# A decoder layer with three token mixers: one small statistics tile grows by 320 bytes, and the tiles allocated behind it move up by as much

## The chip, the core and the metric

The kernel runs on one core of a Trainium2 chip. The metric is the time of one execution on the device, in microseconds (us); lower is better. Before the change it is 323.63 us, the median of three runs (323.2 to 323.89).

## What is computed

One layer over 256 tokens of width 1024, in fp32. Cut to what matters:

```python
h = rmsnorm(x, g_in)
z = h @ w_in                      # one wide projection, then split
ya = moba_attention(rope(mq), rope(mk), mv);  ya = (ya * silu(mg)) @ w_up_moba
yb = dsa_attention(rope(dq), rope(dk), dv, rope(iq), rope(ik), iw);  yb = (yb * silu(dg)) @ w_up_dsa
yc = cross_attention(xq, *split(rmsnorm(mem, g_mem) @ w_mem_kv));    yc = (yc * silu(xg)) @ w_up_cross
g = sigmoid(glog + b_merge)       # three gates
out = rmsnorm(x + (g[0] * ya + g[1] * yb + g[2] * yc) @ w_out, g_final)
```

## The kernel before, in words

**Arithmetic.** Each fp32 operand of a matmul is split into a high and a low half in fp32r (`split_act`, L181 on, for x and mem; `split_weights`, L240 on, for weights), and each product is three matmuls: high by high, high by low, low by high (`product`, L251 on: L254, L255, L256; L280 in `gemm`). A matmul has a stationary operand (128 rows by 128 columns, loaded into TensorE by a LDWEIGHTS; the profile's PEld) and a moving operand that streams past it (128 to 512 columns).

**Order.** The work is a list of some 100 steps. Each step has one block of weights of up to 512 KB: loaded six steps ahead into a `wraw` tile (SP's DMA queue), split three steps ahead by ScalarE (L248, high half) and VectorE (L249, low half) into `whi` and `wlo` tiles, and used by the step's matmuls. The order of steps is written out by hand (`ORDER`), and everything that isn't a weight product (rope, attention, gates, statistics) is hung on a step by `at(...)`. TensorE and GpSimd follow the order of the program text.

**Which operand lies where.** In `gemm_t` (26 blocks of 48 matmuls), in the mq block (`gemm_k`, 96), the two xk blocks (`gemm_kv`, 96) and the up products (`gemm_u`, 12 blocks of 24) the weights are stationary and x, mem or a gated branch output moves, 256 columns at a time: 1248 + 96 + 96 + 288 = 1,728 matmuls. In `gemm` (mv, dv, xv, the two indexer blocks i0 and i1) and in the output product (`out_piece`) it is the other way round: x, mem or u is stationary and the weights move; 512 columns in mv, dv, xv and nearly all of the output product (216 matmuls in all), 264 and 320 in i0 and i1 (48 each).

**Addresses.** On-chip tiles live in pools that are laid out one behind another in the order in which they are opened: `const`, `raws` (raw x and weights), `ws` (split weights), `work` (temporaries), `keep` (the split x and mem, q, k, v, attention outputs, u and its halves). Within a pool each tag gets its slots when it is first used, each slot rounded up to 32 bytes. Counted per partition, this gives for the kernel before:

| what | start, bytes | behind a multiple of 512 |
|---|---|---|
| `cst` (constants, identity) | 16512 | 128 |
| `xr`, `wraw` (raw x, raw weights) | 27648, 35840 | 0 |
| `whi`, `wlo` (split weights) | 52224, 72704 | 0 |
| `nat` | 93184 | 0 |
| `xss` (8 bytes, a slot of 32) | 99328 | 0 |
| `sw` (swapped halves for rope; at the end g_final) | 99360 | 32 |
| `gate`, `t1`, `t2`, `ms` | 103648 to 117984 | 224 |
| `pr`, `pth`, `ptl` (probabilities and their split) | 121184 to 135008 | 352 |
| `xhi`, `xlo` and all else of `keep` | 138272 on | 32 |

The last tile of `keep` ends at byte 226848 of 229376. All `keep` tiles have sizes that are multiples of 512 bytes, so all begin 32 bytes behind a multiple of 512, and every 128-column block of one does as well. A split weight block begins at 0; in i0 (264 columns) its second half begins 1056 bytes on, at 32; in i1 (320 columns) 1280 bytes on, at 256.

**The lines around the change.** `start_stats` (L894 on) is hung on step 6. It squares the rows of x (already loaded into two `keep` tiles) and sums them into `sums`, a tile of two fp32 per partition with the tag `xss`; `rsqrt` (L211 on) turns them into the scale of each row. `sums` is written at L898 and read at L217 once, at 21.6 us.

Of the kernel before, what the change touches and what calls it, by code (L numbers as in the profile page):

```python
# [8 lines left out]
F32 = mybir.dt.float32  # L9
# [5 lines left out]
P = 128  # L15
# [95 lines left out]
def hybrid_layer_kernel(  # L111
# [18 lines left out]
    work = ctx.enter_context(tc.tile_pool(name="work", bufs=2))  # L130
# [83 lines left out]
    def rsqrt(r, ss, nm):  # L214

        v, sd, e = (work.tile([P, 2], F32, name=f"{nm}n{i}", tag=f"n{i}") for i in range(3))
        nc.vector.tensor_scalar(v, ss, 1.0 / D, EPS, op0=OP.mult, op1=OP.add)  # L217
        nc.scalar.activation(sd, v, AF.Sqrt)
        nc.vector.reciprocal(r, sd)
        nc.vector.tensor_tensor(e, r, r, op=OP.mult)  # L220
        nc.vector.tensor_tensor(e, e, v, op=OP.mult)
        nc.vector.tensor_scalar(e, e, -0.5, 1.5, op0=OP.mult, op1=OP.add)
        nc.vector.tensor_tensor(r, r, e, op=OP.mult)
# [668 lines left out]
            x_rows.append(rows)  # L892

    def start_stats():  # L894
        sums = work.tile([P, 2], F32, name="xss", tag="xss", bufs=1)
        for t in range(2):
            junk = work.tile([P, D], F32, name=f"xjunk{t}", tag="sw", bufs=1)
            nc.scalar.activation(junk, x_rows[t], AF.Square, accum_out=sums[:, t : t + 1])  # L898
        rsqrt(x_rstd, sums, "x")
        nc.vector.tensor_scalar_mul(xs_rstd, x_rstd, float(P**-0.5))  # L900
        nc.vector.tensor_copy(ident_r, ident)
        for t in range(2):
            nc.vector.tensor_scalar_mul(tab[:, t, :], tab0[:, t, :], x_rstd[:, t : t + 1])
# [13 lines left out]

    at(LOAD_ROWS, load_rows)
    at(X_STATS, start_stats)
    at(X_STATS, make_bias)  # L920
    at(X_STATS + 2, rstd_rows, x_rstd, rB, "rB")
# [147 lines left out]
```

## Time and profile before

| | |
|---|---|
| median of three runs | 323.63 us (323.2 to 323.89) |
| the profiled execution: its own time, its span | 324.77 us, 323.0 us |
| TensorE busy with matmuls / with weight loads | 313.0 us (97%) / 297.4 us (92%) |
| VectorE, ScalarE, GpSimd busy | 252.1, 202.9, 41.9 us |
| TensorE's granted clock | 0.999 of full |
| bytes moved by DMA, mean rate | 59.45 MB, 184 GB/s |

How to read it: a matmul's recorded duration (0.28 us for 256 columns) covers its way through the array, and the next one starts before it ends, so durations overlap. What one costs when they come back to back is the distance from its start to the next one's start, which the timeline gives to 0.01 us.

### The profile page before, as it was taken

To read this page: it belongs to the slowest core of one execution; us is meant where nothing else is said; L and a number is where in the kernel's file an instruction comes from. 1 tells how busy PE (TensorE), PEld (TensorE's weight loads), DVE (VectorE), ACT (ScalarE), POOL (GpSimd) and SP (SyncE) were. 2 spreads that over 40 slices of the span, in tenths; PEclk is the share of its full clock that TensorE was granted. 3 is DMA by queue.
4 is the path that set the end of the run, shared out by engine and by line. 5 is a ranking of instruction groups with operands and counts; after the bars stand their busy time and mean duration, and the time that the engine had idled before them with its cause. 6 is when DMAs were issued, how large, how long until landed. Compare 5 with 4: busy or idle time off the path is not lost.

```text
span 323.0 us, 6395 instructions
## 1 busy us (share of the span) xinstructions
PE 313.0 (97%) x2442; PEld 297.4 (92%) x2442; DVE 252.1 (78%) x458; ACT 202.9 (63%) x357; POOL 41.9 (13%) x58
## 2 busy tenths in 40 slices
PE   8899999998999999999999999999999999999992
PEld 7699999988999989879999999999999999998882
DVE  3579999899799999988766759998466775677523
ACT  5599674687878545577666588756444546643434
POOL 0001000017202000010200235321000111014011
PEclk9999999999999999999999999999999999999999
DMA  6989886864644446574443434478765666655003
GB/s 202 379 293 333 269 269 194 265 240 124 214 130 127 138 130 210 182 246 131 146 132 117 146 94 162 136 220 302 211 193 189 190 188 205 182 156 188 2 0 130
DMA packets 18368, 59.45 MB, mean 184 GB/s; under 512 B 2209, under 2 KB 2465, under 8 KB 18337
## 3 DMA queue, kind: packets, MB, share of 16 engines
q1 hardware_dynamic: 17760, 57.73, 57.1%
q10 hardware_dynamic: 576, 1.31, 1.0%
q8 instruction: 19, 0.31, 0.5%
q14 instruction: 13, 0.10, 0.1%
HBM read 55.89 MB, written 1.05 MB: 176 GB/s over the span
## 4 chain that ended last, share of the span: by engine, by line
PE 70%; DVE 15%; DMA 5%; ACT 4%; issue 4%; SPq 0%; ACTq 0%; DVEq 0%
DMA w3r<-w_in 3%; DVE wk L498 2%; DMA w25r<-w_in 2%; DVE m L496 1%; PE o_0ps L255 1%; PE o_0ps L256 1%; PE o_0ps L254 1%; DMA w0r<-w_in 1%; PE dya L642 1%; PE i_0ps L280 1%; PE i_1ps L280 1%; PE mv_1ps L280 1%; PE mv_0ps L280 1%; DVE acc L487 1%; PE lg L480 1%
## 5 line engine op out<-in xcount | busy, mean ns | idle before, releaser
L747 POOL TENSOR_TENSOR u<-u,gt 128x512 f32<-128x512 f32 x7 | 9.9, 1411 | 76.7 <-DVE gt L744 76.7
L616 POOL TENSOR_SCALAR dpr<-dpr,dst 128x128 f32<-128x128 f32 (+1 forms) x16 | 6.6, 425 | 84.1 <-DVE dst L614 83.9
L616 POOL TENSOR_SCALAR mpr<-mpr,mst 128x128 f32<-128x128 f32 (+1 forms) x16 | 9.8, 629 | 56.3 <-DVE mst L614 56.3
L734 ACT ACTIVATE gt<-gt,x_first 128x256 f32<-128x256 f32 x24 | 10.9, 501 | 2.7 <-DVE gt L731 2.5
L606 ACT ACTIVATE dpr<-dms,dst 128x128 f32<-128x128 f32 (+1 forms) x16 | 7.1, 446 | 3.6 <-DVE dst L602 3.6
L788 ACT ACTIVATE junk<-xn 128x512 f32<-128x512 f32 (+1 forms) x5 | 2.7, 543 | 8.6 <-DVE xn L786 8.6
L606 ACT ACTIVATE mpr<-mms,mst 128x128 f32<-128x128 f32 (+1 forms) x16 | 7.1, 444 | 1.2 <-DVE mst L602 1.2
L664 ACT ACTIVATE xpr<-xsc,xst,xs_rstd 128x256 f32<-128x256 f32 x8 | 4.4, 560 | 3.4 <-DVE xst L660 3.4
L752 ACT CAST us<-u 128x512 fp32r<-128x512 f32 x4 | 2.5, 624 | 6.2 <-POOL u L747 4.9
L647 ACT COPY dyT<-dya 64x256 f32<-64x256 f32 x8 | 2.9, 367 | 4.2 <-PE dya L642 4.1
L484 ACT ACTIVATE rl<-lg 128x384 f32<-128x384 f32 x8 | 3.9, 485 | 2.7 <-PE lg L480 1.6
L487 DVE SCALAR_TENSOR_TENSOR acc<-rl,iw,acc 128x128 f32<-128x128 f32 (+1 forms) x14 | 5.4, 431 | 0.1
L480 PE MATMUL lg<-ikT,iqT 128*128 128x128 f32 (+1 forms) x32 | 5.1, 282 | 0.1
L968 PE MATMUL warm<-ones 128*128 128x128 f32 x18 | 4.0, 419 | 1.1 <-DVE eps_t L963 1.1
L602 DVE CUSTOM_DVE_ANT_0 mms<-msc,bias_c 128x128 f32<-128x128 f32 (+1 forms) x16 | 5.0, 350 | 0.0
L968 PEld LDWEIGHTS warm<-ones 128*128 128x128 f32 x18 | 3.9, 328 | 1.1 <-DVE eps_t L963 1.1
L648 DVE TENSOR_TENSOR dyT<-dyT,dya 64x256 f32<-64x256 f32 x8 | 3.3, 417 | 1.8 <-ACT dyT L647 1.7
L628 ACT CAST dph<-dtp 128x384 fp32r<-128x384 f32 x8 | 3.8, 479 | 1.4 <-PE dtp L627 1.3
L629 DVE TENSOR_TENSOR dpl<-dtp,dph 128x384 fp32r<-128x384 f32 x8 | 4.4, 553 | 0.4
L602 DVE CUSTOM_DVE_ANT_0 dms<-dsc,sel 128x128 f32<-128x128 f32 (+1 forms) x16 | 4.7, 352 | 0.0
L786 DVE TENSOR_TENSOR xn<-o_0ps,xn 128x512 f32<-128x512 f32 x2 | 1.4, 691 | 4.2 <-PE o_0ps L256 4.2
L498 DVE MATCH_REPLACE8 wk<-m,wk 128x128 f32<-128x128 f32 (+1 forms) x14 | 4.7, 342 | 0.0
(1296 smaller groups left out, 1541.9 us busy)
## 6 DMA issues: line engine op xcount, KB each, us to landing
x_rows<-x SPq DMA_DIRECT2D x2, 512.0 KB, 8.7
eT<-memT SPq DMA_DIRECT2D x4, 256.0 KB, 4.6
xn<-x SPq DMA_DIRECT2D x2, 512.0 KB, 5.5
w0r<-w_in SPq DMA_DIRECT2D x2, 256.0 KB, 3.3
w1r<-w_in SPq DMA_DIRECT2D x2, 256.0 KB, 4.9
xT<-xT SPq DMA_DIRECT2D x2, 256.0 KB, 7.1
w2r<-w_in SPq DMA_DIRECT2D x1, 512.0 KB, 7.3
w3r<-w_in ACTq DMA_DIRECT2D x1, 512.0 KB, 8.7
```

Of the source, the lines that this page charges most:

```text
L280: nc.tensor.matmul(accs[nm][t][:, :n], a[p](k, slice(t * P, (t + 1) * P)), w[q][:, half, :], start=k + i == 0, stop=k + i == nk + 1,)
L480: nc.tensor.matmul(lg[:, c : c + n], q[:, q0:q1], idx["k"][:, j, 0:n], start=j == 0, stop=j == 1)
L487: nc.vector.scalar_tensor_tensor(acc[:, c], rl[:, c], iw[:, t, g : g + 1], (bias_c if g == 0 else acc)[:, c], op0=OP.mult, op1=OP.add,)
L498: nc.vector.match_replace(out=wk[:, c], in_to_replace=m8[t], in_values=src[:, c], imm_value=TAKEN)
L602: nc.vector.tensor_tensor_reduce(out=ms[:, c], in0=sc[:, c], in1=bias()[:, c], op0=OP.add, op1=OP.min, scale=-(HD**-0.5), scalar=3e38, acc ...
L606: big["last_exp"] = nc.scalar.activation(pr[:, c], ms[:, c], AF.Exp, bias=st[:, t : t + 1], scale=-1.0, accum_out=st[:, 2 + t : 3 + t],)
L616: nc.gpsimd.tensor_scalar(pr[:, c], pr[:, c], st[:, 4 + t : 5 + t], 1.0, op0=OP.mult, op1=OP.mult)
L629: nc.vector.tensor_sub(pl, tp[:, 0 : 3 * P], ph.bitcast(F32))
L664: big["last_exp"] = nc.scalar.activation(pr3[:, t, :], sc[:, t, :], AF.Exp, bias=st[:, t : t + 1], scale=xs_rstd[:, t : t + 1], accum_out= ...
L734: nc.scalar.activation(gt[:, f, :], gt[:, f, :], AF.Sigmoid, bias=x_first[:, j : j + 1])
L747: adder.tensor_tensor(u, u, gt, op=OP.add)
L968: nc.tensor.matmul(warm[:, 0:P], ones, ones, start=True, stop=True)
```

## The change

The tile `sums` gets 82 columns instead of 2, and the first two of them are used. It is 328 bytes then, a slot of 352, 320 more than before. All that is allocated behind it moves up by 320 bytes: `sw` and all of `keep` from 32 to 352 behind a multiple of 512; `gate`, `t1`, `t2` and `ms` from 224 to 32; `pr`, `pth` and `ptl` from 352 to 160. What lies before it (constants, raw x, raw and split weights, `nat`) stays. `keep` ends at 227168.

```diff
     def start_stats():
-        sums = work.tile([P, 2], F32, name="xss", tag="xss", bufs=1)
+
+        sums = work.tile([P, 82], F32, name="xss", tag="xss", bufs=1)[:, 0:2]
         for t in range(2):
             junk = work.tile([P, D], F32, name=f"xjunk{t}", tag="sw", bufs=1)
             nc.scalar.activation(junk, x_rows[t], AF.Square, accum_out=sums[:, t : t + 1])
```

## Rows read from the trace of the kernel before

**Rows 1.** The page of the profile: its head and part 1, busy time, share of the span and number of instructions of each engine.
```profile
span 323.0 us, 6395 instructions
PE 313.0 (97%) x2442; PEld 297.4 (92%) x2442; DVE 252.1 (78%) x458; ACT 202.9 (63%) x357; POOL 41.9 (13%) x58
```

**Rows 2.** The page, part 2: the span in 40 slices; tenths of each slice in which PE was busy, and the granted clock in tenths.
```profile
PE   8899999998999999999999999999999999999992
PEclk9999999999999999999999999999999999999999
```

**Rows 3.** Busy time by stretch: the stretch, its length, then busy us (and instructions) of PE, PEld, DVE, ACT, POOL, the granted clock, the DMA engines' busy share and GB/s.
```profile
40.00:80.00 40.00, 38.59 (x324) 37.19 (x323) 38.64 (x82) 27.63 (x50) 6.74 (x11) 1.00 0.70 219
...
240.00:280.00 40.00, 40.00 (x345) 40.00 (x344) 27.78 (x26) 21.69 (x27) 3.87 (x3) 1.00 0.65 191
312.00:323.00 11.00, 4.98 (x34) 4.37 (x32) 3.56 (x10) 5.56 (x13) 1.30 (x1) 0.97 0.25 95
```

**Rows 4.** The longest of the waits of PE: the waiting group, whom it waited for, us in total, times, longest.
```profile
PE warm L968 <- DVE eps_t L963: 1.1, 1, 1.1
```

**Rows 5.** The timeline of PE (start us, us, engine, line, operation, output<-inputs with the moving one first): the first matmul of u21 and the first of the block after it, 24 matmuls later. The moving operand begins at 32, the stationary one at 0.
```profile
269.15 0.28 PE L254 MATMUL u21ps<-xgyh,w83h 128*128 128x256 f32 x1
...
271.95 0.28 PE L254 MATMUL l12ps<-xhi,w84h 128*128 128x256 f32 x1
```

**Rows 6.** The same, in the output product: six matmuls of 512 columns, from the first to the one behind them. Moving at 0, stationary at 32.
```profile
297.15 0.40 PE L254 MATMUL o_0ps<-w93h,us 128*128 128x512 f32 x1
...
298.55 0.40 PE L254 MATMUL o_1ps<-w93h,us 128*128 128x512 f32 x1
```

**Rows 7.** The same, in cross-attention: six matmuls, moving at 224, stationary at 32, and the one behind them.
```profile
183.04 0.28 PE L254 MATMUL xya<-xph,xvh 128*128 128x256 f32 x1
...
183.74 0.28 PE L254 MATMUL xg1ps<-xhi,w54h 128*128 128x256 f32 x1
```

**Rows 8.** The same, in self-attention: two matmuls of 256 columns and two of 128 (the first of each pair is shown), moving at 352, stationary at 32, and what is behind them.
```profile
160.40 0.28 PE L642 MATMUL dya<-dph,dv 128*128 128x256 f32 x1
...
160.64 0.22 PE L642 MATMUL dya<-dph,dv 128*128 128x128 f32 x1
...
160.81 0.41 PE L627 MATMUL dtp<-cst,dpr 128*128 128x128 f32 x2
```

**Rows 9.** The same, in i1 (320 columns, stationary at 32): the first of six matmuls with the moving operand at 0, the first and the last of the six after them with the moving operand at 256.
```profile
62.89 0.30 PE L280 MATMUL i_0ps<-w22h,xhi 128*128 128x320 f32 x1
...
63.77 0.31 PE L280 MATMUL i_0ps<-w22h,xhi 128*128 128x320 f32 x1
...
64.50 0.31 PE L280 MATMUL i_1ps<-w22h,xlo 128*128 128x320 f32 x1
```

**Rows 10.** The same, in i0 (264 columns, stationary at 32): the first matmul of each group of six. The moving operand is at 0 in the first group of a weight block and at 32 in the second.
```profile
41.48 0.28 PE L280 MATMUL i_0ps<-w12h,xhi 128*128 128x264 f32 x1
...
42.20 0.28 PE L280 MATMUL i_0ps<-w12h,xhi 128*128 128x264 f32 x1
...
42.92 0.29 PE L280 MATMUL i_0ps<-w13h,xhi 128*128 128x264 f32 x1
...
43.64 0.28 PE L280 MATMUL i_0ps<-w13h,xhi 128*128 128x264 f32 x1
...
44.37 0.29 PE L280 MATMUL i_0ps<-w14h,xhi 128*128 128x264 f32 x1
...
45.09 0.28 PE L280 MATMUL i_0ps<-w14h,xhi 128*128 128x264 f32 x1
...
45.82 0.28 PE L280 MATMUL i_0ps<-w15h,xhi 128*128 128x264 f32 x1
...
46.54 0.28 PE L280 MATMUL i_0ps<-w15h,xhi 128*128 128x264 f32 x1
...
47.27 0.28 PE L254 MATMUL dq0ps<-xhi,w16h 128*128 128x256 f32 x1
```

**Rows 11.** The same, one indexer head: two matmuls of 128 columns and two of 256, merged into one row, moving and stationary operand both at 32, and the matmul behind them.
```profile
90.32 0.63 PE L480 MATMUL lg<-ikT,iqT 128*128 128x128 f32 x4
90.79 0.28 PE L254 MATMUL dk1ps<-xhi,w29h 128*128 128x256 f32 x1
```

**Rows 12.** Groups of instructions by line and shape on ACT and DVE: busy us, mean ns of one | idle time before. Pairs of like operations whose tiles begin at different places: L248 from 0 to 0, L539 from 32 to 32; L734 in place at 224, L674 in place at 352; L249 all at 0, L753 all at 32.
```profile
L248 ACT CAST w26h<-w26r 128x1024 fp32r<-128x1024 f32 x1 | 1.1, 1055 | 0.2 <-DMA w26r<-w_in 0.2
L539 ACT CAST dkhi<-dkT 128x1024 fp32r<-128x1024 f32 x1 | 1.1, 1054 | 3.0 <-DVE dkT L532 3.0
L734 ACT ACTIVATE gt<-gt,x_first 128x256 f32<-128x256 f32 x24 | 10.9, 501 | 2.7 <-DVE gt L731 2.5
L674 ACT ACTIVATE xpr<-xpr,xst 128x256 f32<-128x256 f32 x8 | 3.6, 504 | 0.4 <-DVE xst L672 0.3
L249 DVE TENSOR_TENSOR w2l<-w2r,w2h 128x512 fp32r<-128x512 f32 x2 | 1.3, 688 | 0.7 <-ACT w2h L248 0.7
L753 DVE TENSOR_TENSOR us<-u,us 128x512 fp32r<-128x512 f32 x4 | 2.7, 684 | 1.8 <-ACT us L752 1.8
```

**Rows 13.** DMA issues: output<-input, queue, operation, count, KB each, median us from issue to landing. The destination of x_rows is at 32, that of w5r, issued between the two, at 0.
```profile
x_rows<-x SPq DMA_DIRECT2D x2, 512.0 KB, 8.7
w5r<-w_in SPq DMA_DIRECT2D x1, 512.0 KB, 7.8
```

## The prediction

> **What bounds the kernel now.** I read the busy times first, then the stretches, then the timeline of TensorE. TensorE is busy for 313.0 of 323.0 us [rows 1], in every slice but the last at eight tenths or more [rows 2], at the upper of its two clock levels, 2.4 GHz (the granted clock is 1.00 in the stretch from 240 to 280 us) [rows 3]. Its longest wait is 1.1 us, before the first matmul [rows 4]. From 240 to 280 us it never pauses: 345 matmuls in 40.00 us. In the stretch from 40 to 80 us VectorE is as full, 38.64 of 40 us, and there TensorE has small gaps (38.59). The last 11 us are the tail, in which TensorE is busy for 4.98 us and the rest is the final normalisation [rows 3]. So the time hangs on the pace at which matmuls follow each other; in part of the first half on VectorE; at the end on a short chain of ScalarE, VectorE and DMA.
>
> That pace is 24 matmuls of 256 columns in 2.80 us, 116.7 ns each or 0.456 ns per column [rows 5], and six of 512 columns in 1.40 us, 233.3 ns each, again 0.456 ns [rows 6]. 2.4 GHz would be 0.417 ns per column, so some 9% is lost to something. The loss grows with the columns streamed, not with the number of weight loads: 10 ns per matmul at 256 columns, 20 ns at 512, with one load in both.
>
> **The change, part by part.** It removes and adds no instruction, no wait and no transfer: `sums` is written and read in the same two columns. All that is different is where tiles lie. Three kinds of access can feel that.
>
> *Matmuls.* The 1,728 matmuls with a stationary weight now have their moving operand at 352 instead of 32, and the stationary one still at 0; in the 216 + 96 others the stationary operand goes from 32 to 352 and the moving one stays. Together they stream 1,728 x 256 + 216 x 512 + 48 x 264 + 48 x 320 = 581,000 columns, which at 0.456 ns is 265 us: here 1% of pace is 2.65 us. What does the place cost? The trace has the moving operand at five places. At 32: 0.456 ns per column [rows 5]. At 0: 0.456 ns [rows 6]. At 224: six matmuls in 0.70 us, 0.456 ns [rows 7]. At 352, the very place to which x goes: two of 256 columns in 0.24 us, 0.469 ns, where the rows' rounding to 0.01 us alone is worth 0.02 ns [rows 8]. At 256: 0.73 us for five steps of 320 columns, 0.456 ns, after 0.88 us for six, 0.458 ns, at 0 [rows 9]. So neither the place of the moving operand nor its distance to the stationary one (32 behind it in rows 5, 32 ahead in rows 6, 192 behind in rows 7, 224 in rows 9) shows in the pace. I take zero. The bounds come from two rows in which both operands begin at the same place. In i0, 24 matmuls with the moving operand at 0 take 4 x 0.72 = 2.88 us, 24 with both at 32 take 0.72 + 3 x 0.73 = 2.91 us: 1.25 ns more on 264 columns, 1% [rows 10]. An indexer head, both operands at 32, takes 0.47 us for 768 columns [rows 11]; the same number and widths of matmuls with the operands apart take 0.41 us [rows 8]. Were 1% put on or taken off all 581,000 columns (0.0047 ns each), that would be 2.75 us; 60 ns per four matmuls on 2,040 would be 31 us. I keep 2.75 us as the bound on either side: the larger figure is from a short group whose order of widths also differs, and the change brings no pair to the same place, since 352 stands against 0.
>
> The Trainium skill, page "SBUF — State Buffer", section "A bandwidth-pool intuition that's wrong (but worth ruling out)", gives TensorE's reads of the moving operand a peak of about 614 GB/s. [...]
>
> *VectorE, ScalarE, GpSimd.* Like operations at different places differ by under 1%: a cast of 128x1024 from 0 to 0 takes 1055 ns, from 32 to 32 it takes 1054; an activation of 128x256 in place takes 501 ns at 224, 504 at 352; a VectorE subtraction of 128x512 takes 688 ns at 0, 684 at 32 [rows 12]. I take zero. Where TensorE runs without a pause even 1% would be hidden under it. Where it isn't, 0.6% (3 of 501 ns, the largest of the three) of the tail's 3.56 + 5.56 + 1.30 = 10.4 us is 0.06 us, and 0.6% of VectorE's 38.64 us between 40 and 80 us is 0.23 us [rows 3], most of which is weight splits that don't move. The bound is 0.3 us on either side.
>
> *DMA.* The weights, nearly all of the bytes, land where they did. What lands elsewhere is x_rows, the swapped halves, and at the end x and g_final. x_rows, at 32, takes 8.7 us; w5r, of the same size and issued between its two parts, 7.8 us at 0 [rows 13]. If place were all of that 0.9 us, it would be a property of 0 against 32. Of 352 there is no row; I take zero. The statistics that wait for x_rows would be late by as much, under matmuls that don't need the row scales before the first evacuations of i0; if that cover were gone it would be 0.9 us, and the same for the load of x before the tail.
>
> **Sum.** 0 + 0 + 0. The profiled execution took 324.77 us, of which the span is 323.0; that is 1.14 us above the median of the three runs, 323.63, and what I forecast is a difference of zero to that median: 323.6 us.
>
> **The rivals.**
> *The two streams meet (slower).* TensorE reads the moving operand of one matmul while it loads the weights of the next. These two are locked to each other in time, so a bad distance would hit every matmul alike. The 1% in i0 and the long indexer head, the only rows with both operands at one place, speak for something of the kind [rows 10, 11]; against it speak the four other distances, all at one pace [rows 5 to 7, 9]. The distances that the change makes, 352 and 160 (352 the other way round, taken within 512), stand in no row. At the price from i0 the time is 323.6 + 2.75 = 326.4 us. It decides from 0.3 ns per matmul of 256 columns on, since 0.65 us over 581,000 columns is 0.0011 ns each. That is less than a timeline of 0.01 us can exclude over 24 matmuls. Chance 0.10.
>
> *The two streams part (faster).* The 9% above the clock's own pace may be just such a meeting, partly or wholly lifted at 352. Wholly, it is 581,000 x 0.039 ns = 22.7 us, 301 us; by the price from i0 it is 2.75 us, 320.9 us. For it: there is a loss of unknown origin on the path that bounds the kernel. Against it: the loss is the same at each of the places, and it goes with columns, though the weight load takes up more of a short matmul than of a long one [rows 5, 6]. Chance 0.12, and in it mostly the small size.
>
> The Trainium skill, same page, section "Who interferes with whom", gives TensorE two independent read ports, one for matmuls and one for weight loads, and says that TensorE and ScalarE wait on no one; by that both rivals have a chance of nothing. The trace agrees at the distances that it has, and no row here shows 352 or 160.
>
> *The slot does not push anything.* If the larger tile left the others where they are, the program would be the one of before, and the time 323.6 us as well. It is part of the likeliest case.
>
> **How the numbers follow.** 0.2% is 0.65 us, about what a measurement of this kernel can tell from no change; the three runs span 0.7 us. The likeliest case, no effect or one within that, has 0.78. It alone covers 323.0 to 324.3 us. To leave out no more than 2 in 10 the range reaches a little into both rivals, by about 0.5 us on either side, which also takes in the 0.3 us of the other engines: 322.5 to 324.8 us. Faster 0.12, same 0.78, slower 0.10.
>
> **What would show it.** In the profile of the changed kernel, u21 should again take 2.80 us for 24 matmuls, six matmuls of the output product 1.40 us, and from 240 to 280 us there should be 345 matmuls. The like pairs on ScalarE and VectorE should stay within 1%, and x_rows near 8.7 us. I am wrong if the 24 matmuls of u21 take 2.78 us or less or 2.82 us or more, which is beyond the rounding and over all columns 2 us, or if the stretch from 240 to 280 us holds 344 matmuls or 347; or if the pace holds and the stretch from 40 to 80 us or the tail moves by more than 0.3 us.

## The result: 1.5% slower, and the profile after

The changed kernel takes 328.21 us (median of four runs, 327.95 to 329.42) against 323.59 us for the kernel before (four runs): a ratio of 1.0146, 95% interval 1.0128 to 1.0165. That is 4.6 us more, outside the range that was given. Its profiled execution took 328.0 us, with a span of 326.2.

The head of the page and part 1, against [rows 1], then the stretches against [rows 3] (columns as there; the last one is cut to the new end of the span).

```profile
span 326.2 us, 6395 instructions
PE 317.9 (97%) x2442; PEld 303.1 (93%) x2442; DVE 252.6 (77%) x458; ACT 202.8 (62%) x357; POOL 42.1 (13%) x58
```

```profile
40.00:80.00 40.00, 39.16 (x324) 37.77 (x323) 37.81 (x84) 26.74 (x50) 7.25 (x12) 1.00 0.69 211
240.00:280.00 40.00, 40.00 (x335) 40.00 (x334) 27.11 (x25) 20.56 (x26) 3.86 (x3) 1.00 0.57 177
312.00:326.20 14.20, 8.20 (x47) 6.94 (x46) 4.96 (x13) 6.29 (x15) 2.57 (x2) 0.88 0.20 74
```

The same 6395 instructions run. VectorE, ScalarE and GpSimd work as long as before, to 0.5 us; TensorE works 4.9 us longer. From 240 to 280 us it is without a pause, at the full clock, as before, but it starts 335 matmuls there instead of 345. The pace itself has changed. The timeline of TensorE, for the blocks of [rows 5], [rows 6], [rows 10] and [rows 7]:

```profile
271.61 0.28 PE L254 MATMUL u21ps<-xgyh,w83h 128*128 128x256 f32 x1
...
274.49 0.28 PE L254 MATMUL l12ps<-xhi,w84h 128*128 128x256 f32 x1
...
300.33 0.40 PE L254 MATMUL o_0ps<-w93h,us 128*128 128x512 f32 x1
...
301.73 0.40 PE L254 MATMUL o_1ps<-w93h,us 128*128 128x512 f32 x1
```

```profile
40.96 0.29 PE L280 MATMUL i_0ps<-w12h,xhi 128*128 128x264 f32 x1
...
46.86 0.28 PE L254 MATMUL dq0ps<-xhi,w16h 128*128 128x256 f32 x1
...
183.35 0.28 PE L254 MATMUL xya<-xph,xvh 128*128 128x256 f32 x1
...
184.05 0.28 PE L254 MATMUL xg1ps<-xhi,w54h 128*128 128x256 f32 x1
```

The 24 matmuls of u21 take 2.88 us instead of 2.80: 120.0 ns each, not 116.7. So do the others in which x, mem or a gated branch moves past the weights, wherever 24 or more such matmuls follow each other without a break. That is beyond both signs of being wrong that the prediction named, 2.82 us for u21 and 344 matmuls in that stretch. The output product still takes 1.40 us for six matmuls of 512 columns. i0 takes 5.90 us for its 48 matmuls, 122.9 ns each, instead of 5.79. Cross-attention, whose moving tile went from 224 to 32 and whose stationary one from 32 to 352, takes 0.70 us for six, as before; its moving operand begins 192 behind the stationary one within 512 in both kernels.

The like pairs on the other engines, against [rows 12], and the load of x, against [rows 13], are where they were:

```profile
L539 ACT CAST dkhi<-dkT 128x1024 fp32r<-128x1024 f32 x1 | 1.1, 1052 | 2.8 <-DVE dkT L532 2.8
L674 ACT ACTIVATE xpr<-xpr,xst 128x256 f32<-128x256 f32 x8 | 3.6, 502 | 0.4 <-DVE xst L672 0.3
L753 DVE TENSOR_TENSOR us<-u,us 128x512 fp32r<-128x512 f32 x4 | 2.7, 681 | 1.8 <-ACT us L752 1.8
```

```profile
x_rows<-x SPq DMA_DIRECT2D x2, 512.0 KB, 8.5
```

**Where along the span the time is lost.** The views of three tiles (line, operation, count: ns min/median/max, first and last start in us), first of the kernel before, then of the changed one:

```profile
L254 PE MATMUL mk1ps<-xhi,w10h x8: 277/279/280, 35.9 to 38.3; 128*128 128x256 f32 x8
L254 PE MATMUL l10ps<-xhi,w56h x8: 277/279/363, 192.0 to 195.6; 128*128 128x256 f32 x8
L254 PE MATMUL u22ps<-xgyh,w91h x8: 278/279/281, 291.6 to 294.0; 128*128 128x256 f32 x8
```

```profile
L254 PE MATMUL mk1ps<-xhi,w10h x8: 279/282/286, 35.2 to 37.7; 128*128 128x256 f32 x8
L254 PE MATMUL l10ps<-xhi,w56h x8: 279/282/364, 192.4 to 195.9; 128*128 128x256 f32 x8
L254 PE MATMUL u22ps<-xgyh,w91h x8: 281/283/285, 294.6 to 297.2; 128*128 128x256 f32 x8
```

Up to mk1 this execution is 0.7 us ahead, because weights came in earlier (w3r 7.4 us from issue to landing, instead of 8.7). From mk1 to l10 it takes 157.2 us instead of 156.1, from l10 to u22 102.2 instead of 99.6, from there to the end 31.6 instead of 31.4. From mk1 on it loses 3.9 us, 2.6 of them from l10 to u22, where TensorE has next to no waits. Of the pair of profiled executions the earlier kernel's lies 1.2 us above its median (324.77 against 323.59) and the changed one's 0.2 below (328.0 against 328.21): they stand 3.2 us apart, where the medians stand 4.6.

### The profile page after: what moved, and what is told of

It is laid out like the page before. It is cut to its first block, busy times and chain, and to the rows that moved or that the text cites. A ratio compares the mean times of both kernels' runs of the same rounds, so it can differ in the third digit from the quotient of the medians.

```text
span 326.2 us, 6395 instructions
## 1 busy us (share of the span) xinstructions
PE 317.9 (97%) x2442; PEld 303.1 (93%) x2442; DVE 252.6 (77%) x458; ACT 202.8 (62%) x357; POOL 42.1 (13%) x58
## 4 chain that ended last, share of the span: by engine, by line
PE 90%; DVE 3%; DMA 2%; ACT 1%; issue 1%; SPq 1%; ACTq 0%
DMA w2r<-w_in 2%; PE i_0ps L280 2%; PE i_1ps L280 2%; PE dv_0ps L280 2%; PE xv_0ps L280 2%; PE dv_1ps L280 2%; PE xv_1ps L280 2%; PE mv_0ps L280 1%; PE mv_1ps L280 1%; PE lg L480 1%; PE o_0ps L256 1%; PE o_0ps L255 1%; PE o_0ps L254 1%; PE dsc L470 1%; PE dya L642 1%; PE mya L642 1%
## 5 line engine op out<-in xcount | busy, mean ns | idle before, releaser
L734 ACT ACTIVATE gt<-gt,x_first 128x256 f32<-128x256 f32 x24 | 10.9, 502 | 2.4 <-DVE gt L731 2.4
```

What stands on the lines that cost most here:

```text
L734: nc.scalar.activation(gt[:, f, :], gt[:, f, :], AF.Sigmoid, bias=x_first[:, j : j + 1])
```

## The experiments

The first theory, PAIR, is the slower rival of the prediction: what counts is how far the moving operand begins from the stationary one. PLACE: the moving operand's own start counts. SURROUNDINGS: something outside TensorE.

**A map of distances.** A kernel of matmuls alone, all alike but for where the two tiles begin:

```diff
+    for m, s, n in CASES:
+        ps = psum.tile([P, 512], F32, name=f"m{m}s{s}n{n}ps", tag="ps", bufs=4)
+        for k in range(REP):
+            nc.tensor.matmul(ps[:, 0:n], st[:, s // 4 : s // 4 + 128], mv[:, m // 4 : m // 4 + n],
+                             start=k == 0, stop=k == REP - 1)
```

> This kernel computes nothing of the layer: it runs 256 groups of ten matmuls of 256 columns in fp32r, the moving tile beginning m and the stationary tile s bytes behind a multiple of 512, m and s each from 0 to 480 in steps of 32, and copies x to the output. Theory PAIR (the distance between the moving operand and the weights that are loaded beside it sets the pace): the time of ten matmuls depends on m - s alone; 1.167 us where m - s is 32, 1.200 us where it is 352. Theory PLACE (the moving operand's own start sets it): it depends on m alone, 1.167 us for m = 32 and 1.200 us for m = 352 at every s. Theory SURROUNDINGS (something else in the layer's kernel, other engines or transfers, sets it): 1.167 us everywhere.

Its timeline (ten matmuls to a row; the name has m and s, and the cost is the distance to the next row's start):

```profile
17.25 1.34 PE L36 MATMUL m32s0n256ps<-mv,st 128*128 128x256 f32 x10
18.43 1.34 PE L36 MATMUL m64s0n256ps<-mv,st 128*128 128x256 f32 x10
...
23.16 1.30 PE L36 MATMUL m192s0n256ps<-mv,st 128*128 128x256 f32 x10
24.31 1.34 PE L36 MATMUL m224s0n256ps<-mv,st 128*128 128x256 f32 x10
...
43.20 1.30 PE L36 MATMUL m224s32n256ps<-mv,st 128*128 128x256 f32 x10
44.34 1.34 PE L36 MATMUL m256s32n256ps<-mv,st 128*128 128x256 f32 x10
```

With s = 0 the quick place is m = 192 (1.15 us for ten, against 1.18 at 32); with s = 32 it is m = 224 (1.14 us). The quick places lie along a diagonal, m - s = 192 and 448 within 512: 26 of its 32 groups take 1.14 to 1.15 us, six 1.17 to 1.18, and no group off it takes less than 1.165. PLACE and SURROUNDINGS fall, and the period looks like 256 bytes. Ten matmuls were too few for the sizes, since each group still carries something of the one before it: 32 gave 1.18 us, not 1.167, and 352 gave 1.19, not 1.200. The two paces of the layer's kernels are not told apart here.

**The same distances in the layer's kernel.** Three kernels that move the weights, or all, instead of x. In the first:

```diff
-    ss = const.tile([P, 8], F32, name="ss")
+    ss = const.tile([P, 88], F32, name="ss")[:, 0:8]
```

> The padding of 320 bytes goes ahead of the weights, not behind them: weights begin at 320, x and what is kept at 352, and their distance is 32 as in the kernel before. PAIR: the 24 matmuls of u21 take 2.80 us, and the time is 323.6 us. PLACE: 2.88 us and 328.2 us, as in the changed kernel, since the moving operand begins at 352. SURROUNDINGS: not settled by this theory; anything between.

In the second the same tile has 56 columns, and `sums` the 82 of the change:

> 192 bytes of padding ahead of the weights and the change's 320 behind them: weights begin at 192, x and what is kept at 32 again (512 further up), and the distance is 32 - 192, which is 352 within 512, as in the changed kernel. PAIR: the 24 matmuls of u21 take 2.88 us, 328.2 us. PLACE: 2.80 us, 323.6 us, since the moving operand begins at 32. SURROUNDINGS: 323.6 us would be no surprise.

In the third `sums` has 130 columns and nothing else is changed:

> The small tile grows so that all behind it moves up by 512 bytes instead of 320; everything begins at the same place within 512 as in the kernel before. PAIR and PLACE: 2.80 us for the 24 matmuls of u21, 323.6 us. If instead a larger period than 512 matters, or the mere growth of the tile, 328 us or anything else than 323.6.

They took 323.52, 328.68 and 323.58 us; ratios to the kernel before 0.9996 (0.9982 to 1.0009), 1.0155 (1.0135 to 1.0176) and 1.0001 (0.9987 to 1.0015). The stretch of the matmul pace, one row for each kernel in this order (columns as in [rows 3]):

```profile
240.00:280.00 40.00, 40.00 (x345) 40.00 (x344) 27.01 (x25) 22.68 (x30) 3.88 (x3) 1.00 0.63 188
```

```profile
240.00:280.00 40.00, 40.00 (x335) 40.00 (x335) 27.17 (x26) 21.02 (x28) 3.86 (x3) 1.00 0.57 176
```

```profile
240.00:280.00 40.00, 40.00 (x346) 40.00 (x345) 26.99 (x25) 22.77 (x30) 3.87 (x3) 1.00 0.60 187
```

x at 352 with the weights at 320 is as quick as before (345 matmuls); x at its old 32 with the weights at 192 is as slow as the change (335). This is PAIR, in the layer, in both directions, and the size of the shift by itself costs nothing.

**A finer map, and two more pushes.** The second map has 24 matmuls to a group. The two kernels of the layer push by 160 and by 64 bytes (`sums` of 42 and of 18 columns).

> Computes nothing of the layer, as the first map: groups of 24 matmuls of 256 columns with the stationary tile at 0 and the moving one at 0 to 504 in steps of 8; then 24 of 512 columns in steps of 32; then two groups of 48 that alternate between two moving and two stationary places, once so that each moving operand is 192 behind its own weights (and 288 or 96 from the weights loaded beside it), once so that it is 192 from the weights loaded beside it (and 288 or 96 from its own). By the first map a distance of 192 or 448 gives 113.8 ns and all others 117 to 120 ns, with a period of 256. BESIDE (the weights that are being loaded meanwhile, those of the next matmul, count): the second of the two last groups runs at 114 ns, the first at 118. OWN: the other way round. If steps of 8 bytes matter there is a narrower best or worst place; if lines of 32 bytes or more matter, steps of 8 within one give the same. At 512 columns the loss by distance is the same few ns per weight load, not twice as much, if it is the load that collides.

> The small tile pushes by 160 instead of 320 bytes: x and what is kept at 192, weights at 0, distance 192, the quickest of the first map. PAIR: the 24 matmuls of u21 take 2.73 us (113.8 ns each), and 1,728 such matmuls gain 1,728 x 2.9 ns = 5.0 us on the kernel before, 318.6 us, somewhat less gained where VectorE holds TensorE up. PLACE: the moving operand at 192 has no reason to be quicker than at 32; 323.6 us.

> Pushed by 64 bytes: x and what is kept at 96, weights at 0, distance 96, which is 352 less 256. PAIR with a period of 256, as the first map has it: 2.88 us for the 24 matmuls of u21 and 328.2 us, as the changed kernel. PAIR with a period of 512: 96 and 352 have nothing in common, and the time may be anything. PLACE: likewise.

The map's timeline:

```profile
26.94 2.96 PE L40 MATMUL m32s0n256ps<-mv,st 128*128 128x256 f32 x24
29.74 3.03 PE L40 MATMUL m40s0n256ps<-mv,st 128*128 128x256 f32 x24
...
84.08 2.90 PE L40 MATMUL m192s0n256ps<-mv,st 128*128 128x256 f32 x24
86.82 3.04 PE L40 MATMUL m200s0n256ps<-mv,st 128*128 128x256 f32 x24
...
141.13 3.04 PE L40 MATMUL m352s0n256ps<-mv,st 128*128 128x256 f32 x24
144.01 3.04 PE L40 MATMUL m360s0n256ps<-mv,st 128*128 128x256 f32 x24
```

At 32 bytes 24 matmuls take 2.80 us, at 352 they take 2.88 us: the two paces of the layer's kernels, with nothing but matmuls on the chip. 192 takes 2.74. Each value from 256 on repeats the one 256 below. At 512 columns distance 0 takes 5.45 us for 24 (227 ns each), 32 takes 5.60 (233 ns); over all distances the spread is some 7 ns at either width, not twice as much at the larger. The two alternating groups at the end ran at 118.3 and 119.9 ns; neither at 114, so they decided nothing between OWN and BESIDE.

The push by 64 bytes, distance 96, took 328.23 us (ratio 1.0127, 1.01 to 1.0155), with 2.88 us for the 24 matmuls of u21, as the changed kernel: the period of 256 holds in the layer. The push by 160, distance 192, was a miss: 323.99 us, ratio 0.9997 (0.9979 to 1.0015), where 318.6 was expected. Its timeline shows why; from the middle of block l10:

```profile
192.79 0.28 PE L254 MATMUL l10ps<-xhi,w56h 128*128 128x256 f32 x1
...
193.81 0.28 PE L254 MATMUL l10ps<-xhi,w57h 128*128 128x256 f32 x1
...
195.98 0.28 PE L254 MATMUL l10ps<-xhi,w57h 128*128 128x256 f32 x1
...
197.04 0.28 PE L254 MATMUL l01ps<-xhi,w58h 128*128 128x256 f32 x1
```

Nine matmuls take 1.02 us (113.3 ns each) ahead of the attention products that are hung into l10, and 1.06 us (117.8 ns) behind them, with the same tiles at the same distance. From there on every block to u22 ran at 117.8 ns. In this execution mk1 to l10 takes 155.0 us (156.1 in the kernel before), l10 to u22 100.5 (99.6), and what the first stretch gains the second nearly loses. So at this distance there are two paces, and something decides which one a stretch keeps.

**What decides it.** A third map, and two layer kernels in which each kind of step has its own distance: the weights begin at a chosen place within a larger tile.

```diff
-        hi = ws.tile(shape, F32R, name=f"w{s}h", tag="whi")
-        lo = ws.tile(shape, F32R, name=f"w{s}l", tag="wlo")
+        o, m = (56 if s in moving else 48), shape[1] * shape[2]      # the second kernel: 8 for 48
+        hi, lo = (
+            ws.tile([P, 1088], F32R, name=f"w{s}{p}", tag=f"w{t}")[:, o : o + m].rearrange(
+                "p (k n) -> p k n", k=shape[1]
+            )
+            for p, t in (("h", "hi"), ("l", "lo"))
+        )
```

(`moving` holds the steps of mv, dv, xv, i0, i1 and the output product; two small statistics tiles lose their second buffer to make room, which puts x and what is kept at 224 within 256. With the weights 48, 8 or 56 columns of 4 bytes into their tile, at 192, 32 or 224, the distance is 32, 192 or 0.)

> Computes nothing of the layer: groups of matmuls of 256 columns. First two kinds of groups that alternate between two moving and two stationary places: in one each moving operand is 32 from its own weights (96 or 224 from those loaded beside it), in the other it is 32 from the weights loaded beside it (96 or 224 from its own). BESIDE: the second runs at 116.7 ns as a constant distance of 32 does, the first does not; OWN: the other way round. Then groups at distance 192 entered from groups at other distances, and after one matmul of another width. In the layer with distance 192 the pace was 113.3 ns in some blocks and 117.8 ns in others, without a change of place: if the pattern that the two streams settle in depends on how the stretch is entered, the groups at 192 here show both paces too, by what stands before them; if the layer's 117.8 ns has another cause, all of them settle at 113.3.

> The weights of the steps in which they move (mv, dv, xv, i0, i1 and the output product) begin at another place within their tiles than the others, so that both kinds of steps have the distance that the map liked: 32 where x moves, 0 where the weights move. PAIR, by the map: 1,728 matmuls stay at 116.7 ns, 216 of 512 columns go from 233.3 to 226.7 ns, 216 x 6.7 ns = 1.4 us less, 322.3 us. If the map does not carry over: no change.

> As the last one, but the distance is 192 where x, mem or a gated branch moves. PAIR, if all these matmuls settle at 113.3 ns: 1,728 x 3.3 ns = 5.8 us less, less what VectorE holds up, and 1.4 us for the others: about 318 us. If the blocks after the last attention step settle at 117.8 ns again, as with the push of 160 bytes: about 322.5 us.

The third map:

```profile
18.49 5.77 PE L57 MATMUL g1m32x96s0x64n256ps<-mv,st 128*128 128x256 f32 x48
24.10 2.05 PE L57 MATMUL g2m8s0n256ps<-mv,st 128*128 128x256 f32 x16
25.99 5.84 PE L57 MATMUL g3m96x32s0x64n256ps<-mv,st 128*128 128x256 f32 x48
31.66 2.04 PE L57 MATMUL g4m8s0n256ps<-mv,st 128*128 128x256 f32 x16
...
48.61 2.89 PE L57 MATMUL g9m192s0n256ps<-mv,st 128*128 128x256 f32 x24
51.34 2.03 PE L57 MATMUL g10m32s0n256ps<-mv,st 128*128 128x256 f32 x16
...
57.85 2.99 PE L57 MATMUL g13m192s0n256ps<-mv,st 128*128 128x256 f32 x24
60.68 2.06 PE L57 MATMUL g14m160s0n256ps<-mv,st 128*128 128x256 f32 x16
...
65.40 2.17 PE L57 MATMUL g16m8s0n256ps<-mv,st 128*128 128x256 f32 x16
67.41 2.99 PE L57 MATMUL g17m192s0n256ps<-mv,st 128*128 128x256 f32 x24
```

At distance 192, 24 matmuls take 2.73 us behind a group at 64 (the row of g9) and 2.83 us behind a group at 96 (g13). Of 36 groups at 192, 21 settled at 113.3 ns and 15 at 117.8, by what stood before them. The groups at distance 8 between them say the same: 16 matmuls take 1.89 us in g2 and 2.01 in g16. Behind a group at 192 that had settled at 113.3 ns they settled at 116.7 (five of five), behind one at 117.8 they settled at 126.7 (six of six). At 64 and 224 no such difference showed. So the pace is a property of the distance and, at some distances, of how the stretch is entered. The alternating groups: 48 matmuls with each moving operand 32 from its own weights take 5.61 us (116.9 ns), with 32 from the next one's weights 5.67 us (118.1 ns); a repeat gave 5.62 and 5.68. That speaks for OWN, by 1.2 ns. But with two places in turn, a matmul's own weights begin where those of the matmul two further on do, so a load two ahead would look the same; this stays open.

Distance 0 for the moving weights alone brought nothing that can be measured: 323.65 us, ratio 1.0004 (0.9985 to 1.0022), where 322.3 was expected. The matmuls of the output product, 72 of the 216, did go from 233.3 to 226.7 ns (six in 1.36 us), and from u22 to the end the profiled execution takes 31.1 us instead of 31.4. Those of dv and xv went to 227 ns too, but from mk1 to l10 it takes 155.9 us, no less than the 155.7 of the kernels in which all moves up or the shift is 512: TensorE waits there in places, and some blocks, mk0 and mk1 whole, settled at 117.8 ns instead of 116.7. How much each of the two takes was not separated. With 192 for the others, the kernel took 321.01 us, ratio 0.9942 (0.9912 to 0.9972): quicker than both kernels of this case. Its twelve runs lie in two groups, seven from 319.94 to 321.10 and five from 323.33 to 324.25 us; the one that was profiled is of the second, and has 117.8 ns from l01 on. That the first group has 113.3 ns there is likely by its time, but no profile of one was taken.

**Forcing the quick pace.** A short matmul ahead of a block, at the start of which the map had always gone to 113.3 ns:

```diff
+            if s in [plan.first[nm] for nm in ['l01']]:      # the second kernel: l01, l02, l03
+                kick = psum.tile([P, 512], F32, name=f"kick{s}", tag="sc", bufs=2)
+                nc.tensor.matmul(
+                    kick[:, 0:96], w[0][:, 0, 0:P], acts["x"][0][:, 0, 0:96], start=True, stop=True
+                )
```

> The last layer kernel (distance 192 where x moves, 0 where the weights move) with one more matmul, of 96 columns into a PSUM tile that nobody reads, ahead of block l01, the first of the long stretch in which TensorE never waits. In the map 96 columns at distance 192 were followed by 113.3 ns in three cases of three, whatever stood before. PATTERN (the way in which the stretch is entered decides which of two paces it keeps): every block from l01 to u22 runs at 113.3 ns in every execution, 24 matmuls of u21 in 2.72 us; on 116.7 ns, 97 us of them gain 2.8 us, with the output product some 320.3 us, and the runs no longer fall into two groups (319.9 to 321.1 and 323.3 to 324.3 in the last kernel). If the two groups have another cause: two groups again.

> The same with such a matmul ahead of l01, l02 and l03. PATTERN: if one is enough, two more cost about 2 x 0.11 us (45 ns and a first matmul of 180 instead of 113) and change nothing else: 320.5 us. If a kick out of the fast pattern can lead into the slow one, blocks behind l02 or l03 run at 117.8 ns and the time is 1 to 3 us more.

One such matmul: 324.15 us, ratio 1.0021 (1.0006 to 1.0036), no gain where 320.3 was expected; its twelve runs form one group, 323.45 to 325.21. Three: 322.07 us, 0.997 (0.9948 to 0.9992), where 320.5 was expected if one kick is enough; nine runs from 321.52 to 322.87 and three from 323.84 to 324.31. The views of tiles in the second kernel (a duration of 276 ns goes with 113.3 ns of pace, 281 with 117.8):

```profile
L261 PE MATMUL l10ps<-xhi,w57l x8: 276/281/288, 194.5 to 197.4; 128*128 128x256 f32 x8
L259 PE MATMUL l01ps<-xhi,w58h x8: 281/281/347, 197.6 to 200.1; 128*128 128x256 f32 x8
L259 PE MATMUL l02ps<-xhi,w63h x8: 281/281/345, 211.8 to 214.4; 128*128 128x256 f32 x8
L259 PE MATMUL l03ps<-xhi,w68h x8: 276/276/348, 226.1 to 228.6; 128*128 128x256 f32 x8
```

In both kernels the first extra matmul came when l10 had just settled at 113 ns and threw it into the slow pace; the second left it there; the third brought the quick one, which then held for all 17 blocks from l03 to u22. The expectation that 96 columns always lead to the quick pace was wrong, for the map had entered them from other distances only. That the way in can set the pace, and that the pace then holds, is shown within one execution. What in the way in decides is not known, and three such matmuls did not bring the quick time in every run.

## Why the prediction was wrong

**What bounds the kernel** was read rightly: the pace of the matmuls is the term that moved, and the time followed it where TensorE is alone. **The cost of ScalarE, VectorE, GpSimd and DMA** at zero was right (1052 for 1054 ns, 681 for 684, 8.5 for 8.7 us).

**The step that failed** is the one for the matmuls: "neither the place of the moving operand nor its distance to the stationary one ... shows in the pace. I take zero." The distance was the right quantity, but the trace has few of its values, and the change made one that isn't among them. In the finer map the pace over distances of 0 to 504 bytes goes from 113.3 to 121.7 ns; 32 has 116.7, and 352 has 120.0. The kernel's own values lay near each other by chance: 192 is one of the quick distances, but the six matmuls of [rows 7] come between other work, and the first six of the map's group at 192 average 116.8 ns as well, before it settles. The reading of 352 from [rows 8] was no help, since there 352 stands against 32, a distance of 320 (2.83 us for 24 in the map: 117.9 ns). Four equal samples were taken for a constant. The hint that was in the rows, 1% in i0 where both operands begin at one place [rows 10], points the same way as the map at 256 columns (120.0 ns at distance 0, 117.9 at 224, the distance of the rest of i0); no map has 264 columns, and at 512 distance 0 is the quickest. It was set aside because the change makes no distance of 0.

**The slower rival** named the quantity that decided, the distance of the two streams, with a chance of 0.10 and 326.4 us; the range ended at 324.8. Its price was too small: 0.0047 ns per column from i0, where the 1,728 matmuls measured 3.33 ns on 256 columns, 0.013 ns per column. They make 1,728 x 3.33 = 5.8 us. The 216 matmuls of 512 columns, costed alike, lost about 1 ns each (24 in the output product take 5.62 us instead of 5.60), some 0.2 us in all. That it is the reads of the two streams that get in each other's way is argued: the runs show that the distance counts, not how.

**The cover** that the prediction gave to VectorE worked the other way as well. From mk1 to l10 there are 720 of the 1,728 matmuls, worth 2.4 us, and 1.1 came through: there TensorE had waited for other engines in places, and a slower TensorE waits less. Its longest waits between 35.5 and 192 us (whom it waited for, us in total, times, longest), first of the kernel before, then of the changed one:

```profile
PE mya L642 <- DVE mpl L629: 1.0, 1, 1.0
PE mBt L913 <- DVE m_rstd L223: 0.4, 1, 0.4
PE xpt L684 <- ACT xpr L674: 0.3, 1, 0.3
```

```profile
PE mya L642 <- DVE mpl L629: 0.8, 1, 0.8
```

The wait of mBt is 0.05 us or less in the two other kernels at distance 32, in which all moves up or the shift is 512; they take 155.7 us from mk1 to l10. Against them 1.5 us came through. So 0.9 to 1.3 us were covered, and 5.8 less that is 4.5 to 4.9 us, an estimate, against 4.6 between the medians. From mk1 to the end the profiled executions of those two kernels take 286.7 us each, and those of the three at 352 or 96 take 291.0 each, 4.3 us more. What the matmuls ahead of mk1 add was not separated from the weights' arrival there, which differs from run to run (mk1 begins at 34.5 to 36.1 us in the profiled executions of the layer).

**The faster rival** supposed that the loss above the clock's own pace is such a meeting of streams. Partly so: distance 192 lifts 116.7 to 113.3 ns in the map. No distance came near the 106.7 ns of 256 columns at 2.4 GHz. The prediction held against this rival that the loss grows with the columns, but its two rows are at different distances. At distance 0 the map has the same loss at both widths, 13.3 ns (120.0 less 106.7 at 256 columns, 226.7 less 213.3 at 512); at 32 it has 10 and 20.

**The Trainium skill**, page "SBUF — State Buffer", section "Who interferes with whom", from which both rivals would have had no chance, says that TensorE waits on no one and reads by two independent ports. The measurement differs: with TensorE alone at work, the distance between its two operands moves its pace from 113.3 to 121.7 ns in the second map. To hold that the rival was possible in spite of the page was right; to give it 0.10 was too little. The figure of 614 GB/s that the prediction takes from the same page, section "A bandwidth-pool intuition that's wrong (but worth ruling out)", is given there for bf16, two bytes a lane; the moving operand of [rows 5] has four, at 1,123 GB/s (256 columns x 128 rows x 4 bytes in 116.7 ns), and no run here has bf16.

## What to carry to other kernels

Where TensorE bounds a kernel with fp32r matmuls, the start of the moving operand less that of the stationary one, within 256 bytes, is a quantity to choose; a tile that grows ahead of one of them can change it, here with 1.5% of the time, so compare two versions of a kernel only with these distances in view. A few equal samples in a trace don't bound a value that isn't among them: a kernel of matmuls alone maps many of them in one run, each as it is entered from the one before. A gain at one distance has to be confirmed in the kernel itself, since the order of its matmuls can settle in another pace.

## What the runs showed of the hardware that was not expected

- The pace at one distance is not one number: at 192 it is 113.3 or 117.8 ns, by how the stretch was entered, and each holds for hundreds of matmuls. At 8 it was 120.0 ns in the second map, and 116.7, 120.0 or 126.7 in the third. At 32 the kernel before and its shifted likes had 116.7, but the kernel in which only the moving weights are at distance 0 had 117.8 in mk0, mk1 and parts of other blocks.
- At 2.4 GHz the settled paces 113.3, 116.7 and 120.0 ns for 256 columns are 272, 280 and 288 periods: 256, one to a column, and 16, 24 or 32 more. Others, 117.8 among them, are averages that are no whole number of periods.
- In steps of 8 bytes, distances that are no multiple of 16 gave 118 to 122 ns in the second map (8 gave other paces in the third); the quickest were 112 and 192 (113.3 once settled), then 16 and 32 (116.7).
